# Where the weight tiles stand in SBUF against the matmuls' right sides: one pad for each stage, and the lower halves at two places in turn

## The chip, the cores and the metric

The kernel runs on one core of one Trainium2 chip. The metric is the device time of one execution in microseconds. The input is one sequence of 256 tokens, all in float32.

## The reference

Two layers, each of three sublayers with an adaptive norm in front: a feed-forward block, a mixer, a feed-forward block. The mixer of layer 0 is a hybrid (RG-LRU beside a chunked SSD), that of layer 1 is an mLSTM.

```python
for layer in range(2):
    mod = (silu(c) @ ada_w[layer] + ada_b[layer])        # shift, scale, gate of 3 sublayers
    h = modulate(x, 0)                                   # rms_norm, scale, shift
    x = x + 0.5 * (1 + gate0) * swiglu(h, w_gate, w_up, w_down)   # 1024 -> 2816 -> 1024
    h = modulate(x, 1)
    y = hybrid_mixer(h, ...) if layer == 0 else mlstm_block(h, ...)
    x = x + (1 + gate1) * y
    h = modulate(x, 2)
    x = x + 0.5 * (1 + gate2) * swiglu(h, ...)
return rms_norm(x, final_norm_g)
```

Nearly all the arithmetic is the product of 256 tokens with weights that are read once: the gate, up and down projections of four feed-forward blocks, and the input and output projections of the two mixers.

## The kernel before

All weights lie in DRAM as one stream of 128x128 tiles in the order of use, 2928 of them, in 366 pieces of 8 tiles (512 KB). `Weights._piece(i)` loads a piece (`wraw`, SP queue), rounds it on ScalarE to float32r (`whi`, the upper half) and subtracts on VectorE (`wlo`, the lower half, what the rounding left). It runs 4 pieces ahead of the use. Six buffers of each half go round in one pool. Activations are kept as two parts in the same way.

A product of a tile is three matmuls with the 256 tokens as columns: upper weights times upper tokens, upper times lower, lower times upper. Two forms exist, and this text calls them narrow and wide.

- Narrow (`multiply`, lines L333, L334, L335; the four output blocks that open a sublayer do the same with 258 columns in L380 to L382): each of the three has its own weight load (128 columns, `LDWEIGHTS`) and 256 columns. 2118 tiles: the gate and up projections (tile names `gu`, `gu_f`), all of the hybrid's (`bc`, `xbc`, `xl`, `z`, `ri`, `gl`, `od1`), the mLSTM's input (`up`, `zz`), and the last of the eight output blocks of the last sublayer.
- Wide (`out_project`, L438 and L440): the upper tile meets both parts of the tokens in one matmul of 512 columns, then the lower tile 256 columns. 810 tiles: the other output projections (`od0`, `od2`, `od3`, `od4`, `od5`; the digit is the sublayer).

The weight load of a matmul can run while the matmul ahead of it runs. In the text an offset is the address of the weight tile that is being loaded, less the address where the right side (the tokens' tile, `hb`, `ph`, `yb`, `ysb`, `ylb` or `xlb`) of the running matmul begins, in bytes within a partition, modulo 512. A tile's row is 512 bytes long and both parts of every right side begin at the same place modulo 512 (`LO_ROW` and the pads see to that), so all tiles of a stage have the same offset, whatever buffer they are in. Tiles named `pad` or `xpad` are never written or read; they only move what is allocated after them. `WIDE` lists the pieces whose lower half is shifted by 64 bytes (`o = 16` elements).

The scheduler of the framework sets the order on each engine, by priorities and by when buffers come free; `ADA_PLAN` spreads 144 further loads and products on VectorE (`ada`, the modulation) over the pieces.

Of the kernel before, what the change touches and what calls it, by code (L numbers as in the profile page):

```python
# [11 lines left out]
F32 = mybir.dt.float32  # L12
# [7 lines left out]
P = 128  # L20
# [36 lines left out]
WIDE = []  # L57
for _i, _n in enumerate((ND * NF, 0, ND * NF, ND * NF, ND * 16, ND * NF)):
    _e = sum(SUB_TILES[:_i + 1])
    WIDE.append(((_e - _n) // PIECE, _e // PIECE))  # L60
LO_ROW = 384


# [6 lines left out]
class Weights:  # L70
# [14 lines left out]
    def _piece(self, i):  # L85
        nc = self.nc
        w = PIECE * P
        raw = self.raw_pool.tile([P, w], F32, tag="wraw", name=f"wraw{i}")
        nc.sync.dma_start(raw, self.src[i])


        o = 16 if any(p <= i < q for p, q in WIDE) else 0
        hi = self.part_pool.tile([P, w], F32R, tag="whi", name=f"whi{i}")
        lo = self.part_pool.tile([P, w + 128], F32R, tag="wlo", name=f"wlo{i}")[:, o:o + w]
        with self.tc.high_priority(offset=self.ahead):
            if i < 2:
                raw_hi = nc.scalar.copy(hi, raw)
                if i == 1:
                    self.tc.add_manual_dep(raw_hi.ins, self.first[1].ins.name, NOSYNC, reason="the first input first")
            else:  # L100
                raw_hi = nc.scalar.copy(hi, raw)  # L101
            self.last = nc.vector.tensor_tensor(out=lo, in0=raw, in1=hi.bitcast(F32), op=ALU.subtract)  # L102
        if i < 2:
            self.tc.add_manual_dep(self.last.ins, self.first[0].ins.name, NOSYNC, reason="the first input first")
        self.parts[i] = (hi, lo)
        self.splits[i] = (raw_hi, self.last)
        for n, ins in self.after.pop(i, ()):
            self._behind(i, n, ins)
# [25 lines left out]
def body(ctx: ExitStack, tc: tile.TileContext, a, out, dbg=None):  # L134
# [4 lines left out]
    xp = ctx.enter_context(tc.tile_pool(name="xp", bufs=1))  # L139
# [30 lines left out]


    hb = xp.tile([P, ND, 2 * LO_ROW], F32R, name="hb")
    xp.tile([P, 48], F32, name="xpad")
    hh, hl = hb[:, :, 0:T + 2], hb[:, :, LO_ROW:LO_ROW + T + 2]
    h = [hb[:, k, 0:2 * LO_ROW].rearrange("p (i t) -> p i t", i=2)[:, :, 0:T] for k in range(ND)]
    hx = [(hh[:, k, :], hl[:, k, :]) for k in range(ND)]
# [16 lines left out]
    for b in range(2):  # L193
        q = fpool.tile([P, D], F32, name=f"xsq{b}")
# [616 lines left out]
    def mlstm_weights(pp, pw):  # L811
        NC = 16

        wc = pp.tile([P, 3, NC, 4], F32, name="wqkv")
        nc.gpsimd.dma_start(wc, a["ml_w"])
        wkr = pw.tile([P, NC, 4, 4], F32, name="wkr")
        nc.gpsimd.dma_start(wkr, a["ml_wkr"])
        bg = pp.tile([P, 8], F32, name="bg")
        nc.gpsimd.dma_start(bg, a["ml_bg"][0:1, :].to_broadcast([P, 8]))
        wqk = pp.tile([P, NC, 4], F32, name="wqk")  # L820
        pr = pw.tile([P, NC, 4, 4], F32, name="wqk_pr")
        nc.vector.tensor_tensor(out=pr, in0=wkr, in1=wc[:, 0].unsqueeze(2).to_broadcast([P, NC, 4, 4]), op=ALU.mult)
        nc.vector.tensor_reduce(out=wqk, in_=pr, axis=AX.X, op=ALU.add)
        wg = []
        for i in range(3):
            r = pw.tile([P, NC, 8, 4], F32, tag="wgr", name=f"wgr{i}")
            nc.gpsimd.dma_start(r, a["ml_wg"][i])
            nc.vector.tensor_tensor(out=r, in0=r, in1=wc[:, i].unsqueeze(2).to_broadcast([P, NC, 8, 4]), op=ALU.mult)
            g = pp.tile([P, NC, 8], F32, name=f"wg{i}")
            nc.vector.tensor_reduce(out=g, in_=r, axis=AX.X, op=ALU.add)  # L830
            wg.append(g)
        wcg, wvg = wg[0], wg[2]
        nc.vector.tensor_tensor(out=wcg, in0=wg[0], in1=wg[1], op=ALU.add)
        return wc, wqk, wcg, wvg, bg
# [214 lines left out]
    for s in range(6):  # L1049
        W.ahead = AHEAD[s]  # L1050
        kind = ("ffn", "hyb", "ffn", "ffn", "ml", "ffn")[s]
        if s == 3:
            pp = outer.enter_context(tc.tile_pool(name="mlp", bufs=1, reuse_waits="tile"))
        with ExitStack() as sc:
            if kind == "ffn":
                fp = sc.enter_context(tc.tile_pool(name=f"ffn{s}", bufs=NF, reuse_waits="tile"))
                fp.tile([P, 56 if s in (2, 5) else 48], F32, name=f"pad{s}", bufs=1)
                during = None
                if s == 3:
                    pw = sc.enter_context(tc.tile_pool(name="mlpw", bufs=1, reuse_waits="tile"))  # L1060
                    weights = []
                    during = lambda: weights.extend(mlstm_weights(pp, pw))
                ys = ffn(s, acc, fp, during)
            elif kind == "hyb":
                sp = sc.enter_context(tc.tile_pool(name="hyb", bufs=1, reuse_waits="tile"))
                sp.tile([P, 120], F32, name="pad1")
                wk = sc.enter_context(tc.tile_pool(name="hybw", bufs=8, reuse_waits="tile"))
                ys, beside = hybrid(s, acc, sp, wk)
            else:
                sp = sc.enter_context(tc.tile_pool(name="ml", bufs=1, reuse_waits="tile"))  # L1070
                sp.tile([P, 48], F32, name="pad4")
                wk = sc.enter_context(tc.tile_pool(name="mlw", bufs=16, reuse_waits="tile"))
                ys = mlstm(s, acc, sp, wk, weights)
            acc = out_project(s, ys, kind == "ffn", beside if kind == "hyb" else None)
        if s == 0:
            first.close()
        if s == 4:
            outer.close()
# [130 lines left out]
```

## Time and profile before

| | before |
|---|---|
| median of 3 runs | 1148.38 us (1145.75 to 1150.41) |
| the profiled execution | 1148.33 us, of which span 1146.6 |
| TensorE busy | 1124.3 us of the span, 98% |
| VectorE busy | 957.8 us, 84% |
| ScalarE busy | 642.6 us, 56% |
| DMA | 236 GB/s of HBM traffic over the span |
| granted TensorE clock, mean | 0.997 |

The span runs from the first to the last instruction; the time of an execution is a little longer. TensorE's matmuls are pipelined: a matmul shows 0.28 us although the next begins 0.12 us after it, so what counts is the distance between starts. The place of a row in the program is read from its line and from the names out<-in.

### The profile page before, as it was taken

The page shows a single profiled execution, that of the slowest core. Times are in us where ns is not written, and L with a number is a line of the kernel's source. Part 1 is how long each engine was busy: PE and PEld are TensorE (multiplying, and loading weights), DVE is VectorE, ACT ScalarE, POOL GpSimd, SP SyncE. Part 2 cuts the span into 40 slices and gives each one's busy share as a digit, 9 for nine tenths or more (in the row PEclk, how much of TensorE's full clock was granted, in tenths as well). Part 3 has the DMA queues.
Part 4 walks back from the last instruction along what each step waited for, and adds up shares of the span by engine and source line. Part 5 has one row for each costly group of instructions (what it writes and reads, how often), then busy time and mean ns, then how long its engine had stood idle before and what let it go on. Part 6 is the DMA issues. An engine that isn't in the chain of part 4 may idle for free.

```text
span 1146.6 us, 21903 instructions
## 1 busy us (share of the span) xinstructions
PE 1124.3 (98%) x8548; PEld 1072.7 (94%) x8548; DVE 957.8 (84%) x1831; ACT 642.6 (56%) x1074; POOL 8.6 (1%) x25
## 2 busy tenths in 40 slices
PE   7999999999999999999999999999999999999997
PEld 6999988999989999999899998889999889999987
DVE  7999899999889798788889888989879988766562
ACT  4465444788976565444554444458765456544452
POOL 0000000000000000000000000000000000000000
PEclk8999999999999999999999999999999999999999
DMA  8999989656655659899849899983532375875561
GB/s 319 349 305 367 373 294 334 204 172 201 198 166 170 203 196 328 297 313 309 276 150 322 291 336 346 328 270 110 156 120 75 117 239 158 266 227 189 183 198 42
DMA packets 75273, 272.25 MB, mean 237 GB/s; under 512 B 8449, under 2 KB 9121, under 8 KB 75170
## 3 DMA queue, kind: packets, MB, share of 16 engines
q1 hardware_dynamic: 74160, 268.99, 69.4%
q0 software_dynamic: 432, 1.10, 0.4%
q8 instruction: 67, 1.10, 0.4%
q10 hardware_dynamic: 578, 0.76, 0.2%
q14 instruction: 36, 0.29, 0.1%
HBM read 269.77 MB, written 1.05 MB: 236 GB/s over the span
## 4 chain that ended last, share of the span: by engine, by line
PE 84%; DVE 8%; DMA 4%; ACT 2%; issue 1%; ACTq 0%; DVEq 0%; SPq 0%
PE od L438 13%; PE gu L335 13%; PE gu L334 13%; PE gu L333 13%; PE od L440 7%; DMA wraw<-in_wst_dram 4%; DVE wlo L102 3%; ACT whi L101 1%; PE gu_f L380 1%; PE gu_f L382 1%; PE up L335 1%; PE up L334 1%; PE up L333 1%; PE gu_f L381 1%; PE od L333 1%
## 5 line engine op out<-in xcount | busy, mean ns | idle before, releaser
L101 ACT CAST whi<-wraw 128x1024 fp32r<-128x1024 f32 x364 | 380.6, 1049 | 289.1 <-DMA wraw<-in_wst_dram 164.8
L102 DVE TENSOR_TENSOR wlo<-wraw,whi 128x1024 fp32r<-128x1024 f32 x366 | 446.9, 1222 | 100.5 <-ACT whi L101 97.1
L334 PE MATMUL gu<-hb,whi 128*128 128x256 f32 x1312 | 365.9, 280 | 0.1
L335 PE MATMUL gu<-hb,wlo 128*128 128x256 f32 x1312 | 365.9, 280 | 0.0
L333 PE MATMUL gu<-hb,whi 128*128 128x256 f32 x1312 | 362.4, 280 | 1.5 <-ACT hb L349 1.5
L334 PEld LDWEIGHTS gu<-hb,whi 128*128 128x128 f32 x1312 | 246.9, 188 | 0.4 <-DVE hb L350 0.3
L335 PEld LDWEIGHTS gu<-hb,wlo 128*128 128x128 f32 x1312 | 246.8, 188 | 0.0
L333 PEld LDWEIGHTS gu<-hb,whi 128*128 128x128 f32 x1312 | 244.7, 188 | 2.0 <-ACT hb L349 2.0
L438 PE MATMUL od<-ph,whi 128*128 128x512 f32 x682 | 234.0, 391 | 2.4 <-DVE ph L327 2.4
L440 PE MATMUL od<-ph,wlo 128*128 128x256 f32 x682 | 189.0, 277 | 0.0
L219 DVE SCALAR_TENSOR_TENSOR ada<-ada,cact 128x1024 f32<-128x1024 f32 x144 | 175.0, 1219 | 0.1
L438 PEld LDWEIGHTS od<-ph,whi 128*128 128x128 f32 x682 | 128.1, 188 | 29.6 <-DVE ph L327 2.7
L440 PEld LDWEIGHTS od<-ph,wlo 128*128 128x128 f32 x682 | 128.0, 188 | 0.0
L326 ACT CAST ph<-fg 128x256 fp32r<-128x256 f32 x88 | 35.2, 406 | 89.7 <-DVE fg L469 89.4
L445 DVE SCALAR_TENSOR_TENSOR x<-od,gate,x 128x256 f32<-128x256 f32 x87 | 41.6, 481 | 23.0 <-PE od L440 11.8
L327 DVE TENSOR_TENSOR ph<-fg,ph 128x256 fp32r<-128x256 f32 x88 | 36.7, 422 | 12.3 <-ACT ph L326 12.3
L438 PE MATMUL od<-yb,whi 128*128 128x512 f32 x128 | 45.1, 396 | 0.0
L468 ACT ACTIVATE fg<-gu 128x256 f32<-128x256 f32 x82 | 30.6, 377 | 15.2 <-PE gu L335 15.1
L333 PE MATMUL zz<-hb,whi 128*128 128x256 f32 x128 | 37.4, 292 | 0.0
L335 PE MATMUL zz<-hb,wlo 128*128 128x256 f32 x128 | 37.0, 289 | 0.0
L334 PE MATMUL zz<-hb,whi 128*128 128x256 f32 x128 | 36.8, 287 | 0.0
L440 PE MATMUL od<-yb,wlo 128*128 128x256 f32 x128 | 36.0, 282 | 0.0
(407 smaller groups left out, 1887.8 us busy)
## 6 DMA issues: line engine op xcount, KB each, us to landing
wraw<-in_wst_dram SPq DMA_DIRECT2D x366, 512.0 KB, 4.3
ada<-in_adaT_dram SPq DMA_DIRECT2D x144, 512.0 KB, 5.4
xn<-in_x_dram SPq DMA_DIRECT2D x2, 512.0 KB, 4.0
wgr<-in_ml_wg_dram POOLq DMA_DIRECT2D x3, 256.0 KB, 5.7
out_dram<-res ACTq DMA_DIRECT2D x2, 128.0 KB, 2.3
out_dram<-res SPq DMA_DIRECT2D x2, 128.0 KB, 2.1
out_dram<-res SPq DMA_DIRECT2D x1, 256.0 KB, 2.5
out_dram<-res ACTq DMA_DIRECT2D x1, 256.0 KB, 2.6
```

The costliest lines, as they stand in the source:

```text
L101: raw_hi = nc.scalar.copy(hi, raw)
L102: self.last = nc.vector.tensor_tensor(out=lo, in0=raw, in1=hi.bitcast(F32), op=ALU.subtract)
L219: nc.vector.scalar_tensor_tensor(out=raw, in0=raw, scalar=1.0, in1=cact, op0=ALU.mult, op1=ALU.mult, accum_out=mods[s][:, m:m + 1])
L326: nc.scalar.copy(hi, src)
L327: nc.vector.tensor_tensor(out=both[:, 1, :], in0=src, in1=hi.bitcast(F32), op=ALU.subtract)
L333: m = nc.tensor.matmul(dst, wh, both[:, 0, :], start=start, stop=False, skip_group_check=True)
L334: nc.tensor.matmul(dst, wh, both[:, 1, :], start=False, stop=False, skip_group_check=True)
L335: nc.tensor.matmul(dst, wl, both[:, 0, :], start=False, stop=stop, skip_group_check=True)
L438: nc.tensor.matmul(bank, wh, both.rearrange("p i t -> p (i t)"), start=(k == 0), stop=False, skip_group_check=True)
L440: nc.tensor.matmul(sums[0], wl, both[:, 0, :], start=False, stop=(k == len(rhs) - 1), skip_group_check=True)
L445: nc.vector.scalar_tensor_tensor(out=xs_t[d], in0=part, scalar=g[:, d:d + 1], in1=xs_t[d], op0=ALU.mult, op1=ALU.add)
L468: nc.scalar.activation(g, b[:, 0:T], AF.Silu)
```

## The change

The pad behind the tokens' tile grows by 256 bytes, so that everything after it, the weights' buffers among it, moves by 256 bytes modulo 512. The hybrid's own pads follow, one of them new (`pad2`), which places the right side `xlb` like the others. The lower half gets a shift that depends on whether the piece's number is odd, and the last two pieces no longer count as wide.

```diff
 for _i, _n in enumerate((ND * NF, 0, ND * NF, ND * NF, ND * 16, ND * NF)):
     _e = sum(SUB_TILES[:_i + 1])
     WIDE.append(((_e - _n) // PIECE, _e // PIECE))
+WIDE[-1] = (WIDE[-1][0], WIDE[-1][1] - 2)
 LO_ROW = 384
@@ Weights._piece
-        o = 16 if any(p <= i < q for p, q in WIDE) else 0
+        o = 16 + 64 * (i % 2) + (0 if any(p <= i < q for p, q in WIDE) else 16)
         hi = self.part_pool.tile([P, w], F32R, tag="whi", name=f"whi{i}")
         lo = self.part_pool.tile([P, w + 128], F32R, tag="wlo", name=f"wlo{i}")[:, o:o + w]
@@ body
-    xp.tile([P, 48], F32, name="xpad")
+    xp.tile([P, 112], F32, name="xpad")
@@ body, the hybrid's pools
-                sp.tile([P, 120], F32, name="pad1")
+                sp.tile([P, 184], F32, name="pad1")
                 wk = sc.enter_context(tc.tile_pool(name="hybw", bufs=8, reuse_waits="tile"))
+                wk.tile([P, 104], F32, name="pad2", bufs=1)
```

The offsets in the built programs, in bytes modulo 512:

| matmuls | tiles | upper, before | upper, now | lower, before | lower, now (even, odd piece) |
|---|---|---|---|---|---|
| narrow, right side `hb`, `ysb`, `ylb` | 2080 | 192 | 448 | 192 | 64, 320 |
| narrow, right side `xlb` | 16 | 96 | 448 | 96 | 64, 320 |
| narrow, last output block, `ph` | 22 | 448 | 448 | 0 | 64, 320 (16 tiles); 256 (6 tiles) |
| wide, `ph` and `yb` | 810 | 448 | 448 | 0 | 0, 256 |

The number of instructions on each engine is the same, and the order on TensorE, VectorE and the SP queue too. The new pad takes the hybrid's small buffers off memory that was used earlier, and so three small instructions move. On ScalarE at the program's start (`cact` is the conditioning vector after Silu, `x` the transposed input, `dg` the first diagonal tile of the SSD's skip), before:

```order
L190 ACTIVATE cact<-c_107 128x512
L190 ACTIVATE cact<-c_110 128x512
L201 COPY x<-xT_118 128x512
L201 COPY x<-xT_124 128x512
L201 COPY x<-xT_130 128x512
```

and now, where `dg` waits for the column table `cols`:

```order
L191 ACTIVATE cact<-c_107 128x512
L191 ACTIVATE cact<-c_110 128x512
L754 ACTIVATE dg_3846<-ident,cols 128x128
L202 COPY x<-xT_118 128x512
L202 COPY x<-xT_124 128x512
L202 COPY x<-xT_130 128x512
```

The diagonal tile now stands ahead of the copies of x. Its old place on ScalarE is at the end of the first sublayer (`wdt`, `wdh` are the small weights of the SSD's time step), before:

```order
L101 CAST whi_2398<-wraw_2396 128x1024
L753 ACTIVATE dg_3845<-ident,cols 128x128
L316 ACTIVATE sq_o_7_2442<-x 128x256
L363 ACTIVATE hb<-x,scale_1922 128x256
L101 CAST whi_2420<-wraw_2418 128x1024
L619 ACT_TABLE_LOAD
L619 ACTIVATE hv<-hv 128x16
L101 CAST whi_2491<-wraw_2489 128x1024
L599 CAST wdh<-wdt 128x128
```

and now:

```order
L102 CAST whi_2398<-wraw_2396 128x1024
L600 CAST wdh<-wdt 128x128
L317 ACTIVATE sq_o_7_2442<-x 128x256
L364 ACTIVATE hb<-x,scale_1922 128x256
L102 CAST whi_2420<-wraw_2418 128x1024
L620 ACT_TABLE_LOAD
L620 ACTIVATE hv<-hv 128x16
L102 CAST whi_2492<-wraw_2490 128x1024
```

The cast of the small weights has taken the diagonal tile's place, since its load no longer waits. On GpSimd (POOL), whose queue issues that load, before:

```order
L204 AFFINE_SELECT tri<-ones 128x128
L595 DMA hv<-in_ssd_hv_dram 128x32
L597 DMA wdt<-in_wdt_dram 128x128
L638 MEMSET stk 48x256
L817 DMA wkr<-in_ml_wkr_dram 128x256
```

and now:

```order
L205 AFFINE_SELECT tri<-ones 128x128
L598 DMA wdt<-in_wdt_dram 128x128
L596 DMA hv<-in_ssd_hv_dram 128x32
L639 MEMSET stk 48x256
L818 DMA wkr<-in_ml_wkr_dram 128x256
```

The load of `wdt` has passed that of `hv`, which still waits for memory of the first sublayer, and so is issued at the program's start.

## The prediction

> **What bounds the kernel now.** I read the page's busy shares and the chain of work that ended last, then tables of busy time for chosen stretches, then single start times of matmuls in order of time.
>
> ```profile
> PE 1124.3 (98%) x8548; PEld 1072.7 (94%) x8548; DVE 957.8 (84%) x1831; ACT 642.6 (56%) x1074; POOL 8.6 (1%) x25
> ...
> PE 84%; DVE 8%; DMA 4%; ACT 2%; issue 1%; ACTq 0%; DVEq 0%; SPq 0%
> ```
>
> TensorE is busy for 98% of the span and makes 84% of the chain: the time is a count of matmuls times the distance from one start to the next. So the question is that distance. By stage, for the matmuls of one tile name alone (stretch, its length, then TensorE's busy time with the number of matmuls; the last three columns are granted clock, DMA share and GB/s):
>
> ```profile
> 70.00:130.00 60.00, 60.00 (x512) 60.00 (x511) 4.59 (x11) 4.17 (x11) 1.00 0.98 367
> 980.00:1070.00 90.00, 90.00 (x767) 90.00 (x766) 6.66 (x16) 6.01 (x16) 1.00 0.69 219
> ```
> ```profile
> 150.00:190.00 40.00, 40.00 (x230) 35.06 (x229) 5.08 (x11) 1.00 0.95 336
> 530.00:570.00 40.00, 40.00 (x237) 35.52 (x236) 4.81 (x10) 1.00 0.88 301
> 915.00:945.00 30.00, 30.00 (x173) 26.23 (x172) 5.58 (x12) 1.00 0.74 228
> ```
>
> The first two are narrow matmuls (256 columns) of the feed-forward layers: 60/512 is 117 ns each and 90/767 is 117 ns, at clock 1.00, whether the DMA share is 0.98 or 0.69. The other three are wide pairs (512 then 256 columns): 40/230 is 174 ns a matmul, 348 ns a pair; 40/237 is 169 ns, 338 a pair; 30/173 is 347 a pair. The same program line with equal offsets modulo 512 takes two different times in different stages at the same clock. Single starts show it. Narrow, first the usual spacing, then a shorter one:
>
> ```profile
> 979.16 0.28 PE L333 MATMUL gu<-hb,whi 128*128 128x256 f32 x1
> 979.28 0.28 PE L334 MATMUL gu<-hb,whi 128*128 128x256 f32 x1
> 979.39 0.28 PE L335 MATMUL gu<-hb,wlo 128*128 128x256 f32 x1
> 979.51 0.28 PE L333 MATMUL gu<-hb,whi 128*128 128x256 f32 x1
> ```
> ```profile
> 965.11 0.28 PE L333 MATMUL gu<-hb,whi 128*128 128x256 f32 x1
> 965.23 0.28 PE L334 MATMUL gu<-hb,whi 128*128 128x256 f32 x1
> 965.34 0.28 PE L335 MATMUL gu<-hb,wlo 128*128 128x256 f32 x1
> 965.45 0.28 PE L333 MATMUL gu<-hb,whi 128*128 128x256 f32 x1
> ```
>
> A tile's three matmuls take 0.35 us there and 0.34 here; over longer stretches 353 ns (3 x 117.7) and 340 (3 x 113.3). Wide, the first output projection and the second feed-forward's:
>
> ```profile
> 160.14 0.28 PE L440 MATMUL od<-ph,wlo 128*128 128x256 f32 x1
> 160.26 0.40 PE L438 MATMUL od<-ph,whi 128*128 128x512 f32 x1
> 160.49 0.28 PE L440 MATMUL od<-ph,wlo 128*128 128x256 f32 x1
> ```
> ```profile
> 560.21 0.28 PE L440 MATMUL od<-ph,wlo 128*128 128x256 f32 x1
> 560.33 0.39 PE L438 MATMUL od<-ph,whi 128*128 128x512 f32 x1
> 560.55 0.28 PE L440 MATMUL od<-ph,wlo 128*128 128x256 f32 x1
> ```
>
> 350 ns a pair against 340, to the end of each stage. So there is a loss of about 4 ns in a narrow matmul and 10 in a pair, which comes and goes with the phase in which a weight load meets the running matmul. The change moves that meeting, nothing else.
>
> **The change part by part.**
>
> *Order.* TensorE, VectorE and the SP queue keep their order to the instruction. Three small ones move, since the pad takes the hybrid's buffers off older ones. On ScalarE the first diagonal tile (0.40 us) goes from 202.03 to the start, between the second Silu and the first copy of x, and waits there for the column table:
>
> ```profile
> 1.34 5.08 DMA cols<-in_cols_dram
> 6.23 0.60 ACT L190 ACTIVATE cact<-c 128x512 f32<-128x512 f32 x1 [1.11 <-PE c L189]
> 7.27 0.59 ACT L201 COPY x<-xT 128x512 f32<-128x512 f32 x1 [0.45 <-PE xT L200]
> 202.03 0.40 ACT L753 ACTIVATE dg<-ident,cols 128x128 f32<-128x128 f32 x1
> wdt<-in_wdt_dram POOLq DMA_DIRECT2D x1, 64.0 KB, 4.2
> ```
>
> The table lands at 6.42, the Silu ends at 6.83, the copy starts at 7.27: 0.40 fits into 0.44, cost 0. If the table landed late, its lateness would stand in front of the copies, which the first matmuls need. The cast of the small weights moves up into the place that the tile left. On POOL the load of wdt (64 KB) passes that of hv and so starts at about 1.8 us, beside the table's load (226 KB, in the 5.08 us above): 64/226 of that, 1.4 us, is the bound above, 0 the one below; I take 0.2, since the table is only one of many loads then in flight.
>
> *Wide tiles* (810). Upper offset stays 448; the lower goes from 0 to 0 and 256 in turn. Bounds: the two stages at 350 (304 tiles) go to 340, -3.0 us; the three at 340 (506 tiles) go to 350, +5.1. I take 0, because both spacings hold with these offsets now.
>
> *Narrow tiles* (2118, of which 2096 stood at 192 for both halves, 16 of them at 96). Now upper 448, lower 64 and 320. The nearest rows with the upper at 448 are the 22 tiles of the very last output block, which are narrow and had upper 448, lower 0:
>
> ```profile
> 1132.23 0.28 PE L333 MATMUL od<-ph,whi 128*128 128x256 f32 x1
> 1132.35 0.28 PE L334 MATMUL od<-ph,whi 128*128 128x256 f32 x1
> 1132.47 0.28 PE L335 MATMUL od<-ph,wlo 128*128 128x256 f32 x1
> 1132.59 0.28 PE L333 MATMUL od<-ph,whi 128*128 128x256 f32 x1
> 1132.70 0.28 PE L334 MATMUL od<-ph,whi 128*128 128x256 f32 x1
> 1132.82 0.28 PE L335 MATMUL od<-ph,wlo 128*128 128x256 f32 x1
> 1132.94 0.28 PE L333 MATMUL od<-ph,whi 128*128 128x256 f32 x1
> 1133.05 0.28 PE L334 MATMUL od<-ph,whi 128*128 128x256 f32 x1
> 1133.16 0.28 PE L335 MATMUL od<-ph,wlo 128*128 128x256 f32 x1
> 1133.29 0.28 PE L333 MATMUL od<-ph,whi 128*128 128x256 f32 x1
> ```
>
> The next weights load while a matmul runs. Under L333 the load at 448 runs: 0.12, 0.11, 0.11, mean 113 ns, the free value. Under L334 the load at 0: 0.12, 0.12, 0.11, mean 117. Under L335 again 448: 0.12, 0.12, 0.13, mean 123. Sum 353, as at 192. Unlike there, the losses are not even: upper after upper is free, and the loss sits at the lower load and the one behind it. In the wide pairs of 340 the load at 448 runs under a narrow matmul without loss (560.21 to 560.33). So I take 448 as a place that costs nothing unless the lower load before it has upset the phase, and 0 as one that does. For 64 and 320 no row exists. Bounds for a tile: 3 x 113.3 = 340 with no loss anywhere; 113 + 123 + 123 = 359 with the longest step at the lower load and its successor. I take 344.6, two free steps and one lower step of 118, the mean of 113 and 123: of all values seen under a narrow matmul it is the usual one. That is 8.6 ns less than 353.2.
>
> *How much reaches the end.* 1312 tiles of the feed-forward loop (164 output blocks of 8) and 96 that open it run with TensorE always busy: 1408 x 8.6 ns = 12.1 us. The other 688, in the hybrid and the mLSTM, stand in stretches where TensorE waits for others too (tables of all instructions; columns TensorE, weight loads, VectorE, ScalarE):
>
> ```profile
> 64.00:137.00 73.00, 73.00 (x623) 73.00 (x621) 69.45 (x110) 38.09 (x59) 0.00 (x0) 1.00 0.98 359
> 203.00:372.00 169.00, 165.01 (x1350) 156.90 (x1349) 153.60 (x349) 135.22 (x265) 0.00 (x0) 1.00 0.59 185
> ```
>
> VectorE is busy for 153.60 of 169.00 there; I count half, 3.0 us. What is late next is supply: in 64 to 137 VectorE is busy for 69.45 of 73 and the DMA engines for 0.98. A stretch shorter by 8.6/353 would be 71.2, VectorE at 98%; I take 1.1 us off for waits that then show. Sum: -12.1 - 3.0 + 1.1 + 0.2 = -13.8. The profiled execution took 1148.33 us (span 1146.6 and 1.73 around it), the median of the runs is 1148.38, so no correction: 1134.5, in round numbers 1135.
>
> What can be told from no change is about 0.5%, 5.7 us: the three runs before span 4.7.
>
> **The rivals.**
>
> *Nothing to tell (1148).* Every meeting costs the same on average wherever it falls. For it: 192 gives 353 a tile, 448 with 0 gives 353, and 96 gives no less (the first and last of five starts in a row, three rows left out):
>
> ```profile
> 302.39 0.28 PE L334 MATMUL ri<-xlb,whi 128*128 128x256 f32 x1
> ...
> 302.87 0.28 PE L335 MATMUL ri<-xlb,wlo 128*128 128x256 f32 x1
> ```
>
> 0.48/4 is 120. Against it: 340 exists in the same rows, so the average isn't forced. Its time is 1148.3 + 0.2, with up to -3.0 or +5.1 from the wide tiles, still inside 0.5%. A rule gives the same time by another way: the Trainium skill, "TensorE: Matmul & The Clock Gate", Part 2, the step on LDWEIGHTS, says that loading the next tile's weights takes no SBUF read bandwidth from the running matmul, as the two have ports of their own. By it no address would matter, and no loss should come and go; of the 0.27 below, I give 0.05 to this reason alone. The trace doesn't bear that out: the 128x512 matmul takes 0.40 us at 160.26 and 0.39 at 560.33, at one clock.
>
> *All free (1118).* The two lower places keep the phase where it costs nothing, everywhere: 2096 x 13.2 ns = 27.7 us if the hybrid's share counts fully, and 3.0 of the wide tiles: 1148.3 - 30.7. For it: steps of 113 ns are seen at 965 even with offsets that usually lose them. Against: supply, by the 69.45 of 73.
>
> *Slower (1159).* One mechanism: the lower load at 64 or 320 meets the matmul at its worst, and the upper load behind it starts out of phase, as under L335 in the last block. Both steps then take 122 and the first 114, 358 a tile: 2096 x 4.9 = 10.3 us. It decides from 355.9 a tile on (5.7 us/2096 tiles above 353.2). For it: 0.13 at 1133.16, with lower at 0. Against: these rows then begin each tile with a free step, which makes up for it.
>
> *The change not taking effect* is excluded: the built program holds every narrow upper load at 448 past its right side.
>
> **How the numbers follow.** Forecast 0.36, all free 0.14, nothing 0.27, slower 0.23. Faster by over 0.5% is the first two, 0.50; within 0.27; slower 0.23. The forecast's own range comes from the lower step: at 123 a tile takes 349.6, 3.6 less, and the same sum ends at 1142; at 115 it takes 341.6 and ends at 1129. Since cases of both signs hold most of the chance, the range runs from all free, 1117, to just past slower, 1160; I leave out about 0.12, for tiles above 358 (up to the bound of 359) together with wide tiles that turn slow, and for a late column table on top.
>
> **What the profile of the changed kernel would show.** Right: matmuls of 60 us of the feed-forward loop rise from 512 towards 525 (512 x 353.2/344.6), with steps of 0.11 under L334 (then L335) and more under the lower load only. All free: 530 or more. Nothing: 510 to 514. Slower: fewer than 508, with the longest steps at the lower load. Wide: pairs of 340 or 350; a switch at every eighth tile would show that the two lower places differ. The start is right if the diagonal tile stands in the gap before 7.27 and the copy of x has not moved. Wrong would be the forecast if 64 and 320 act unlike each other, one free and one at the worst, since a mean over pieces then hides both, or if VectorE in the first layer can't follow.

## The result and the profile after

| | before | after |
|---|---|---|
| median of 16 runs each | 1148.02 us (1144.45 to 1151.9) | 1142.61 us (1133.27 to 1146.1) |
| ratio after/before, 95% interval | | 0.9937, 0.9913 to 0.9961 |
| the profiled execution, and its span | 1148.33 us, 1146.6 | 1143.54 us, 1141.8 |

The change makes the kernel faster by 0.63%, 5.4 us. Two readings of the profile matter: the gain is not spread over all narrow tiles, and one part of it is given back. First the page's lines that answer to those of before, busy shares and chain:

```profile
PE 1116.2 (98%) x8548; PEld 1064.0 (93%) x8548; DVE 957.6 (84%) x1831; ACT 642.6 (56%) x1074; POOL 8.7 (1%) x25
...
PE 73%; DVE 14%; DMA 6%; ACT 4%; issue 3%; ACTq 0%; SPq 0%
```

TensorE's share of the chain fell from 84% to 73%, VectorE's rose from 8% to 14%: at some place TensorE now waits for others. The same span by sublayer, each from the start of its first matmul to the start of the next sublayer's first (the last one to the end of the span):

| | before, us | after, us | difference |
|---|---|---|---|
| up to the first weight matmul | 15.03 | 14.56 | -0.47 |
| 1, feed-forward | 188.29 | 187.03 | -1.26 |
| 2, hybrid | 187.48 | 188.69 | +1.21 |
| 3, feed-forward | 189.95 | 191.03 | +1.08 |
| 4, feed-forward | 188.43 | 189.37 | +0.94 |
| 5, mLSTM | 183.19 | 181.15 | -2.04 |
| 6, feed-forward | 194.23 | 189.97 | -4.26 |

(The program counts sublayers from 0, so sublayers 1, 3, 4 and 6 of this table have the tile names `gu0`/`od0`, `gu2`/`od2`, `gu3`/`od3` and `gu5`/`od5`. From here on I use these names.)

In this execution nearly all of the gain comes from the last sublayer. Tables of busy time for the `gu` matmuls alone say why (stretch, length, TensorE's busy time with the count of matmuls, then weight loads, VectorE, ScalarE, clock, DMA share, GB/s). Before, in `gu0`, `gu2`, `gu3` and `gu5`:

```profile
30.00:130.00 100.00, 100.00 (x851) 100.00 (x851) 7.49 (x19) 6.91 (x19) 1.00 0.96 350
430.00:500.00 70.00, 70.00 (x597) 70.00 (x596) 4.98 (x12) 4.89 (x13) 1.00 0.90 314
610.00:690.00 80.00, 80.00 (x682) 80.00 (x681) 5.39 (x13) 4.87 (x13) 1.00 0.90 317
980.00:1060.00 80.00, 80.00 (x682) 80.00 (x681) 5.82 (x14) 5.26 (x14) 1.00 0.70 225
```

and after:

```profile
30.00:130.00 100.00, 99.93 (x852) 99.74 (x851) 7.50 (x19) 6.80 (x19) 1.00 0.94 345
430.00:500.00 70.00, 70.00 (x591) 70.00 (x590) 4.98 (x12) 4.88 (x13) 1.00 0.87 311
610.00:690.00 80.00, 80.00 (x708) 80.00 (x707) 5.39 (x13) 4.85 (x13) 1.00 0.90 321
980.00:1060.00 80.00, 80.00 (x709) 80.00 (x707) 6.22 (x15) 5.62 (x15) 1.00 0.68 228
```

Before, each loop has one matmul in 117 ns. After, `gu3` and `gu5` have one in 113 (80/708), but `gu2` has one in 118.4 (70/591), at the same offsets, clock and program line. Single starts show the two spacings. In `gu2`:

```profile
439.76 0.28 PE L334 MATMUL gu<-hb,whi 128*128 128x256 f32 x1
...
440.48 0.28 PE L334 MATMUL gu<-hb,whi 128*128 128x256 f32 x1
```

Six steps, 0.72 us, 120 ns. In `gu3`:

```profile
640.06 0.28 PE L334 MATMUL gu<-hb,whi 128*128 128x256 f32 x1
...
640.74 0.28 PE L334 MATMUL gu<-hb,whi 128*128 128x256 f32 x1
```

Six steps, 0.68 us, 113 ns. The mean distance of the starts is 118.9 ns in `gu2` from its third piece on (the first two contain waits), and 113.4 over the whole of `gu3` and `gu5`. `gu0` changes over within the loop: it runs at 113.3 from its sixth piece to an interruption in its fifteenth, and at 118.9 from there to its end. Even and odd pieces, so lower at 64 and at 320, do not differ in either.

`gu3` is 4.2 us shorter than before (108.71 us, was 112.95), and the output projection behind it, `od3`, is 5.2 longer (67.59, was 62.41). The list of waits of TensorE, and its starts in order of time:

```profile
PE od L439 <- DVE ph L328: 5.7, 2, 3.3
```
```profile
709.31 0.28 PE L441 MATMUL od<-ph,wlo 128*128 128x256 f32 x1
711.99 0.56 PE L439 MATMUL od<-ph,whi 128*128 128x512 f32 x1 [2.40 <-DVE ph L328]
712.34 0.41 PE L441 MATMUL od<-ph,wlo 128*128 128x256 f32 x1
716.09 0.79 PE L439 MATMUL od<-ph,whi 128*128 128x512 f32 x1 [3.33 <-DVE ph L328]
716.68 0.41 PE L441 MATMUL od<-ph,wlo 128*128 128x256 f32 x1
716.90 0.63 PE L439 MATMUL od<-ph,whi 128*128 128x512 f32 x1
```

TensorE stands idle for 5.7 us (2.4 in before), waiting for the token parts `ph` of the next output rows. Then it runs at half the clock: a wide matmul takes 0.63 us instead of 0.39, and the table gives the granted clock beside it:

```profile
712.60:719.00 6.40, 3.07 (x10) 2.52 (x10) 5.74 (x9) 2.32 (x5) 0.00 (x0) 0.50 0.92 294
```

What `ph` waits for on its way stands in the rows of ScalarE and VectorE just ahead: the rounding of a piece waits for its load, the lower half waits for the rounding, and the tokens' parts stand behind it in VectorE's order.

```profile
707.81 1.05 ACT L102 CAST whi<-wraw 128x1024 fp32r<-128x1024 f32 x1 [2.63 <-DMA wraw<-in_wst_dram]
```
```profile
708.89 1.23 DVE L103 TENSOR_TENSOR wlo<-wraw,whi 128x1024 fp32r<-128x1024 f32 x1 [1.31 <-ACT whi L102]
```

So the place where the kernel got faster is followed by one that waits for its supply, and the wait costs twice, once as idle time and once as half clock. The first output projection, `od0`, went from 61.48 us to 59.74 (a wide pair in 340 ns instead of 350); `od2`, `od4` and `od5` kept theirs within 0.2 us.

### The profile page after: what moved, and what is told of

It reads as the page before. It is cut to its first block, busy times and chain, and to the rows that moved or that the text cites. A ratio compares the mean times of both kernels' runs of the same rounds, so it can differ in the third digit from the quotient of the medians.

```text
span 1141.8 us, 21905 instructions
## 1 busy us (share of the span) xinstructions
PE 1116.2 (98%) x8548; PEld 1064.0 (93%) x8548; DVE 957.6 (84%) x1831; ACT 642.6 (56%) x1074; POOL 8.7 (1%) x25
## 4 chain that ended last, share of the span: by engine, by line
PE 73%; DVE 14%; DMA 6%; ACT 4%; issue 3%; ACTq 0%; SPq 0%
PE od L439 15%; PE gu L335 9%; PE gu L334 9%; PE gu L336 9%; PE od L441 8%; DVE wlo L103 5%; DMA wraw<-in_wst_dram 5%; DVE ada L220 3%; ACT whi L102 2%; DVE hb L351 1%; DMA wgr<-in_ml_wg_dram 1%; PE od L334 1%; PE up L335 1%; PE up L336 1%; DVE ht L348 1%
## 5 line engine op out<-in xcount | busy, mean ns | idle before, releaser
L335 PE MATMUL gu<-hb,whi 128*128 128x256 f32 x1312 | 365.8, 280 | 0.1
L334 PE MATMUL gu<-hb,whi 128*128 128x256 f32 x1312 | 360.2, 279 | 1.6 <-ACT hb L350 1.5
L334 PEld LDWEIGHTS gu<-hb,whi 128*128 128x128 f32 x1312 | 245.1, 189 | 2.3 <-ACT hb L350 2.1
L335 PEld LDWEIGHTS gu<-hb,whi 128*128 128x128 f32 x1312 | 246.8, 188 | 0.3 <-DVE hb L351 0.3
L328 DVE TENSOR_TENSOR ph<-fg,ph 128x256 fp32r<-128x256 f32 x88 | 36.7, 422 | 12.9 <-ACT ph L327 12.8
L334 PE MATMUL zz<-hb,whi 128*128 128x256 f32 x128 | 37.2, 290 | 0.0
L335 PE MATMUL zz<-hb,whi 128*128 128x256 f32 x128 | 36.8, 288 | 0.0
L350 ACT ACTIVATE hb<-ht,shift 128x256 fp32r<-128x256 f32 x48 | 22.6, 505 | 24.2 <-DVE ht L348 24.2
```

Source lines behind the costliest of these rows:

```text
L328: nc.vector.tensor_tensor(out=both[:, 1, :], in0=src, in1=hi.bitcast(F32), op=ALU.subtract)
L334: m = nc.tensor.matmul(dst, wh, both[:, 0, :], start=start, stop=False, skip_group_check=True)
L335: nc.tensor.matmul(dst, wh, both[:, 1, :], start=False, stop=False, skip_group_check=True)
```

## The experiments

Three questions: which part of the change makes the gain, what decides between 113 and 118 ns, and what `od3` waits for. Places are offsets as in the table of the change. Each experiment's runs were compared with runs of the kernel before on the same chip; loops are read from one profiled execution of each.

### Without the turn between two places (lo_one_place)

```diff
-        o = 16 + 64 * (i % 2) + (0 if any(p <= i < q for p, q in WIDE) else 16)
+        o = 16 if any(p <= i < q for p, q in WIDE) else 32
```

> The changed kernel with the lower halves at one place (64 narrow, 0 wide) instead of two in turn; upper stays at 448. Theory of the lock (with the upper at 448 a narrow stage keeps one of two spacings, 113.3 or 118.9 ns, from its beginning on, and the turn between places has no part in it): each of the four feed-forward loops shows one of these two values, time 1133 to 1146, median within 4 us of the changed kernel. Rival, the turn frees the stage: without it every loop stays at one value of 117.7 or more, time 1147 or more.

Measured: 1140.31 us against 1149.65, ratio 0.9931 (0.9911 to 0.9951). `gu3` and `gu5` take 108.71 us as with the change, `gu2` 114.68, `gu0` 122.72 (126.70 with the change). The gain is there without the turn. The theory that a loop keeps its spacing from its beginning on fails in `gu0`, which went from 113 to 119 and back to 113.

### Without the move of the upper weights (upper_192)

The pads of before, the lower weights as in the change:

```diff
-    xp.tile([P, 112], F32, name="xpad")
+    xp.tile([P, 48], F32, name="xpad")
-                sp.tile([P, 184], F32, name="pad1")
+                sp.tile([P, 120], F32, name="pad1")
-                wk.tile([P, 104], F32, name="pad2", bufs=1)
```

> The changed kernel with the three pads of before: upper narrow loads at 192 again, lower at 320 and 64 in turn, wide as in the changed kernel. Theory that the upper place matters: no feed-forward loop keeps 113.3, all are at 117.5 to 118, time 1147 to 1150. Rival, the lower place matters: loops at 113.3 appear as in the changed kernel, time 1133 to 1146.

Measured: 1139.31, ratio 0.9926 (0.99 to 0.9952). The `gu` rows:

```profile
30.00:130.00 100.00, 99.91 (x876) 99.45 (x875) 7.49 (x19) 6.97 (x20) 1.00 0.97 349
430.00:500.00 70.00, 70.00 (x620) 70.00 (x619) 5.25 (x13) 4.49 (x12) 1.00 0.89 311
```

876 where before had 851, 620 where it had 597. The move of the upper weights from 192 to 448, which the prediction built on, is not needed: upper 192 with lower 64 and 320 gives as much. What the change and this run share is the new place of the lower weights. The two upper places are 256 bytes apart, so this run does not say that the upper place is without effect; the scans below take other ones.

### Modulation loads spread out (ada_spread)

```diff
-    (2, (6, 60), range(64, 96)), (3, (6, 60), range(96, 136)), (5, (6, 40), range(136, 144)),
+    (2, (4, 64), range(64, 100)), (3, (1, 66), range(100, 136)), (5, (6, 40), range(136, 144)),
```

Four of the 40 loads of sublayer 3 go to sublayer 2, and the other 36 are spread out.

> The changed kernel with the modulation loads of sublayers 2 and 3 spread thinner (36 each over 60 and 65 pieces instead of 32 and 40 over 54). Theory of supply (the loop of sublayer 3 at 113.3 outruns its weights, and the output projection behind it gives the gain back): the wait of TensorE at the start of that projection falls from 5.7 us to under 2.5 and the half clock behind it is gone, also where the loop runs at 113.3; median 2 us or more under the changed kernel. Rival, the wait comes from the order of the evacuation alone: it stays above 5 us where the loop is at 113.3, median as the changed kernel's.

Measured: 1138.44, ratio 0.991 (0.9877 to 0.9944). `od3` takes 59.73 us behind a `gu3` at 113.4 ns, with no wait inside and no half clock. But the four blocks that open that sublayer take 15.24 us, 2.9 longer: that early loads are in the way there is an argument, not shown. The interval overlaps that of the change (0.9913 to 0.9961), so that this version beats it is not shown either, nor whether the loads or VectorE's products of them had been late.

### The places one after the other (scan1, scan2, scan3)

The right side is moved inside its row so that each sublayer has another upper place; the lower place moves on every five pieces:

```diff
+SCAN = ((124, 2), (190, 3), (304, 5))
+        for p, s in SCAN:
+            if p <= i < p + 40:
+                o = ((64 * ((i - p) // 5)) - 448 + 4 * SHIFT[s]) % 512 // 4
```

scan1 has the upper at 448, 0 and 192 in `gu2`, `gu3` and `gu5`, scan2 at 64, 320 and 128; scan3 has it at 192 in all three and moves the lower by 32 bytes, by 8, and by 64 in falling order.

> The changed kernel with the right side shifted within its row and the lower halves moved every 5 pieces, in three feed-forward loops: upper at 448 in sublayer 2, at 0 in sublayer 3, at 192 in sublayer 5, and in each the lower at 0, 64, 128 up to 448, 5 pieces each. Theory that the upper place decides: with 448 spacings of 113.3 appear for several lower places, with 192 none lasts (117 to 119 throughout), with 0 unknown. Rival, the pair of places decides: single lower places give 113.3 in each of the three loops. Rival, places don't matter and only chance does: each loop keeps one spacing over all its lower places.

> Right side shifted by sublayer so that the upper stands at 64 (sublayer 2), 320 (3), 128 (5); the lower moves on by 64 bytes every five pieces, from 0 to 448. Theory (period of 256 bytes, equal places 117.8): the pattern repeats after four places in each loop, 320 reads like 64, and the place equal to the upper gives 117.8. Rival (distance modulo 512 matters): 64 and 320 differ. One-look time about 1140 to 1150.

> Upper at 192 in all three loops. Sublayer 2: lower in steps of 32 bytes from 0 to 224; sublayer 3: in steps of 8 from 32 to 88; sublayer 5: in steps of 64 in falling order, 448 to 0. Theory (the place sets the spacing, history only draws between two): sublayer 5 gives 113.3 or 118.9 at 320 and 64, 117.8 or 115.5 at 384 and 128, 117.8 elsewhere; within 32 bytes around 64 nothing changes. Rival (the order in which places come sets the spacing): falling order gives other values at the same places, up to 120.

Measured (one execution each): 1143.2, 1144.6 and 1144.8 us. The rows of scan1 for the upper at 192, with the lower at 64, 128 and 192 (12 us each):

```profile
974.00:986.00 12.00, 12.00 (x108) 12.00 (x107) 0.83 (x2) 0.75 (x2) 1.00 0.82 268
988.00:1000.00 12.00, 12.00 (x106) 12.00 (x106) 0.83 (x2) 0.79 (x3) 1.00 0.78 252
1002.00:1014.00 12.00, 12.00 (x104) 12.00 (x104) 0.83 (x2) 0.76 (x2) 1.00 0.66 219
```

and of scan2 for the upper at 64, with the lower at 128, 192, 256 and 448:

```profile
436.00:448.00 12.00, 12.00 (x104) 12.00 (x104) 0.83 (x2) 0.75 (x2) 1.00 0.82 302
450.00:462.00 12.00, 12.00 (x108) 12.00 (x107) 0.83 (x2) 0.75 (x2) 1.00 0.94 333
464.00:476.00 12.00, 12.00 (x105) 12.00 (x103) 0.83 (x2) 0.78 (x3) 1.00 0.89 308
506.00:518.00 12.00, 12.00 (x109) 12.00 (x108) 0.83 (x2) 0.74 (x2) 1.00 0.91 317
```

A count of 12 us is good to one in a hundred only; the mean distance of the starts over the last four pieces of a place gives, in ns a matmul, with both places taken modulo 256 (the first place of `gu2` without the piece that contains waits):

| upper | lower 0 | lower 64 | lower 128 | lower 192 |
|---|---|---|---|---|
| 0 | 120.0 | 117.8 | 119.1 | 117.8 |
| 64 | 117.8 | 117.8 | 118.2 | 113.3 |
| 128 | 118.3 | 117.8 or 118.7 | 118.7 | 116.7 or 120.0 |
| 192 | 117.8 | 113.3 or 118.9 | 115.5 or 117.8 | 117.8 |

The first theory of scan1, that the upper place decides, is refuted: in its loops the upper at 448 had 113.3 at no lower place, and the upper at 192 had it at two. Nor does the distance of the two places alone decide, since upper 0 with lower 128 and upper 64 with lower 192 are equally far apart and take 119.1 and 113.3; both count, from the right side.

In scan2 `gu2` (upper 64) and `gu3` (upper 320) have the same mean in each of their last 35 pieces, to a tenth of a nanosecond, so 256 bytes make no difference there. `gu5` (upper 128) does not bear the theory out: lower places 256 bytes apart gave 117.8 and 118.7 (64 and 320), 116.7 and 120.0 (192 and 448). Whether 256 bytes matter there or the loop entered these places differently is not told apart.

The other two cells with two values, upper 192 with lower 64 and with lower 128, had them at exactly the same offsets in different loops: 113.3 in `gu5` of scan1 and 118.9 in scan3, 115.5 and 117.8. So a pair of places does not always fix the spacing. In scan3 the falling order gave the values of the rising one at every place but three, all in these two cells: lower at 320 and 64 took 118.9 (113.3 in scan1), and lower at 128 took 117.8 (115.5). That the order decides, as the rival had it, is not shown, because `gu2` of scan3, in rising order, took 118.9 at 64 too. From 32 to 88 in steps of 8 every place but 64 gave 117.8, and 64 gave 118.9, so the expectation that nothing changes there was wrong: 8 bytes beside 64 the spacing is another.

The pair of upper 64 with lower 192 (modulo 256) is the only one that went to 113.3 all four times it was met, each time out of a spacing of 117.8 or more.

### The two halves at one place modulo 256 (same_place)

The change, with the narrow lower weights at 192 and 448 in turn:

```diff
-        o = 16 + 64 * (i % 2) + (0 if any(p <= i < q for p, q in WIDE) else 16)
+        o = 64 * (i % 2) + (16 if any(p <= i < q for p, q in WIDE) else 64)
```

> The changed kernel with the narrow lower weights at 192 and 448 in turn, so that they stand at the upper weights' place modulo 256. Theory (what counts is the distance of the two places modulo 256, and the upper place alone does nothing): the gain goes; narrow steps 117.8 ns in all three feed-forward loops (112.9 us each), od3 about 62.4, time 1148 (1144 to 1152). Rival (upper 448 itself is the gain): 113.4 in one or two loops, 1139 to 1143 as with the change.

Measured: 1148.31 against 1148.17, ratio 1.0001 (0.9983 to 1.0019). The gain is gone with the upper weights still at 448. The order of the instructions on every engine is that of the change, so the place of the lower weights is the cause. In the profiled execution, at 1146.0 us the shortest of ten, `gu0` stands at 117.8 after its start, and of the other loops `gu2` alone kept 113:

```profile
430.00:500.00 70.00, 70.00 (x620) 70.00 (x619) 4.98 (x12) 4.85 (x13) 1.00 0.89 313
610.00:690.00 80.00, 80.00 (x682) 80.00 (x681) 5.41 (x13) 4.89 (x13) 1.00 0.87 317
980.00:1060.00 80.00, 80.00 (x682) 80.00 (x681) 5.82 (x14) 5.63 (x15) 1.00 0.66 220
```

So equal places, too, can hold 113 through a loop: the theory's step from equal places to 117.8 is right for two of its three loops, and what the places set is a tendency there.

### Upper 192 and a gentler spread (both)

upper_192 with `(2, (5, 64), range(64, 99)), (3, (5, 66), range(99, 136))` in `ADA_PLAN`.

> Upper 192 with lower 320 and 64 in turn (so the pads of before), and the modulation vectors of sublayers 2 and 3 given out over pieces 5 to 64 and 5 to 66, where they stood over 6 to 60. Theory: a loop draws 113.4 or 118.9, and with the vectors spread od3 keeps 60 us after a short gu3 loop instead of 67; 1134 to 1142, 1137 expected, below the change alone by 2 to 5. Rival (the supply is short anyway, the spread only moves the wait): od3 stays at 66 or od2 or the opening of sublayer 3 grows by as much, 1139 to 1143.

Measured: 1142.36, ratio 0.9954 (0.9937 to 0.9972), at the rival's end. `gu2`, `gu3` and `gu5` are at 113.4, but `od3` waits 4.1 us and takes 65.71, `od2` takes 63.37 (59.75 with the change) and the opening of `gu3` 13.76. Loads moved by a few pieces only moved the wait here; what ada_spread gained in `od3` did not come back here.

### What od3 waits for (ada_no_load, ada_short)

The change, once without the 40 loads of modulation weights of the sublayer of `od3`, once with the loads but a short product:

```diff
-        nc.sync.dma_start(raw, a["adaT"][b])
+        src = cact if 96 <= b < 136 else raw
+        if src is raw:
+            nc.sync.dma_start(raw, a["adaT"][b])
```
```diff
+        n = 16 if 96 <= b < 136 else D
-        nc.vector.scalar_tensor_tensor(out=raw, in0=raw, scalar=1.0, in1=cact, ...
+        nc.vector.scalar_tensor_tensor(out=raw[:, 0:n], in0=raw[:, 0:n], scalar=1.0, in1=cact[:, 0:n], ...
```

> The changed kernel without the 40 loads of modulation weights in sublayer 3 (it multiplies another vector in their place, times zero, so that part of the computation is left out; VectorE's instructions stay). Theory (the loads are what is late in od3: the DMA engines are the limit): after a gu3 loop of 108.7 us od3 takes 60 instead of 67.6, no half clock there, about 1135. Rival (VectorE is the limit): od3 stays at 66 to 68, about 1143.

> The changed kernel with VectorE's multiplication of the 40 modulation weights of sublayer 3 cut to 16 of 1024 columns (that part of the computation is left out); their loads stay. VectorE's work there falls by 40 x 1.1 us. Rival (VectorE is the limit): od3 60, about 1135. Theory (DMA): od3 stays at 66 to 68, about 1143.

Measured: 1135.2 and 1143.9 us. In both `gu3` takes 108.71 us as with the change. `od3` takes 59.73 us without the loads and 65.83 with the short product. ScalarE's waits for the weights' load in the 52 us up to the stall, without the loads and with the short product (total, times, longest):

```profile
ACT whi L102 <- DMA wraw<-in_wst_dram: 2.1, 3, 1.2
```
```profile
ACT whi L102 <- DMA wraw<-in_wst_dram: 15.2, 12, 3.5
```

With the change it was 10.6 in 9 times. The stretches of `od3` (all instructions; columns TensorE, weight loads, VectorE, ScalarE, POOL, clock, DMA share, GB/s), in the same order:

```profile
702.00:762.00 60.00, 60.00 (x357) 53.08 (x355) 50.54 (x77) 28.91 (x38) 2.57 (x4) 1.00 0.66 220
```
```profile
705.00:771.00 66.00, 63.26 (x355) 55.07 (x354) 44.52 (x85) 31.39 (x42) 2.61 (x4) 0.97 0.86 308
```

Without the loads VectorE has its full work, 50.54 of 60, and nobody waits. So the loads are needed for the stall. That VectorE's products have no part is not shown. With the short product its busy time falls to 44.52 of 66, and TensorE still waits for `ph`, but 2.7 us in place of 5.7. Waits and half clock (what the wide pairs longer than 360 ns took beyond 340, added up) cost `od3` 7.9 us with the change, 2.7 in before and 4.6 here; another 1.5 of the 65.83 us are later wide pairs at 350 ns in place of 340. The rows of VectorE with the change show how the two meet. From 708.89, the end of its wait for the late rounding shown above, it works without idle time until it has made the second `ph` that TensorE waits for. A product stands right ahead of that one, as another did at 710.36 ahead of the first:

```profile
714.47 1.22 DVE L220 SCALAR_TENSOR_TENSOR ada<-ada,cact 128x1024 f32<-128x1024 f32 x1
715.62 0.42 DVE L328 TENSOR_TENSOR ph<-fg,ph 128x256 fp32r<-128x256 f32 x1
```

Late loads start the stall, and VectorE then works off what has piled up. The wait is named after VectorE, since `ph` is made there behind the halves of late weights.

### The pair that returns (upper_320)

The change with pads smaller by 32 elements, so the upper at 320 and the lower at 192 and 448, which modulo 256 is 64 and 192:

```diff
-    xp.tile([P, 112], F32, name="xpad")
+    xp.tile([P, 80], F32, name="xpad")
-                sp.tile([P, 184], F32, name="pad1")
+                sp.tile([P, 152], F32, name="pad1")
```

> Upper weights 320 bytes past the right side in place of 448, lower at 192 and 448 in turn (pads smaller by 32 floats); modulo 256 that is 64 and 192, the pair that went to 113.3 in both loops where the lower had been moved there. Theory (this pair leads back to 113.3 from wherever it starts, the change's pair holds whichever it starts in): 113.3 in all feed-forward loops and the first layer 122.7 us, od3 again 66 to 68; time 1134 (1130 to 1139), below the change alone, and a narrower spread of runs. Rival (also drawn at the start of a loop): loops at 118 or more in some stages, 1139 to 1145.

Measured: 1136.54 against 1146.51, ratio 0.9927 (0.9903 to 0.9952).

```profile
30.00:130.00 100.00, 99.90 (x873) 99.21 (x872) 7.46 (x19) 7.24 (x20) 1.00 0.96 347
430.00:500.00 70.00, 70.00 (x620) 70.00 (x620) 4.96 (x12) 4.88 (x13) 1.00 0.90 314
610.00:690.00 80.00, 80.00 (x708) 80.00 (x707) 5.78 (x14) 5.22 (x14) 1.00 0.89 324
980.00:1060.00 80.00, 80.00 (x708) 80.00 (x708) 6.20 (x15) 5.62 (x15) 1.00 0.68 221
```

All four loops are at 113. In `gu0` two pieces were thrown to 118 and the pieces behind them came back to 113; with the change the same loop, once thrown from 113 to 119, stayed there to its end, and in lo_one_place, at the change's pair, it was thrown from 119 to 113 and stayed there. `od3` gives 4.6 us back again (66.97), 1.5 of it because its wide pairs ran at 350 ns in place of 340 behind the wait. The runs range over 9.1 us, with the change over 12.8, which is not the narrow band I expected. The intervals of the two ratios overlap, so the time does not show that this pair beats the change's. The loops speak for it: in upper_320 and late_eight all four are at 113.3. Of the seven profiled executions at the change's pair modulo 256 (the change, lo_one_place, upper_192, ada_spread, both, ada_no_load, ada_short) `gu3` and `gu5` came to 113.3 in all, `gu2` in three, and `gu0` ended there in three.

### Eight loads later (late_eight)

upper_320, with `(3, (6, 62), range(96, 128)), (4, (10, 28), range(128, 136))` in `ADA_PLAN`: eight of the 40 loads go to the mLSTM.

> Upper weights at 320, lower at 192 and 448 in turn, and eight of the 40 modulation loads of sublayer 3 given to sublayer 4 (32 over pieces 6 to 62 there, eight over pieces 10 to 28 of the mLSTM, which has DMA shares of 0.3 to 0.5). Theory (the loads of the modulation weights are what od3 is late by): od3 60 to 62 us instead of 67, the mLSTM 0 to 3 longer for eight more instructions on VectorE (10 us there), time 1131 (1128 to 1137). Rival (the mLSTM's VectorE pays it all back): od3 60, the mLSTM longer by 6 or more, 1136 to 1140.

Measured: 1134.46 against 1150.16, ratio 0.9895 (0.9855 to 0.9935), the lowest time of all. `od3` takes 64.55 (66.97 in upper_320), with one wait:

```profile
PE od L439 <- DVE ph L328: 3.1, 1, 3.1
```

and the mLSTM, from its first matmul to the next sublayer's first, 184.45 us (180.75 in upper_320). So between these two executions `od3` gains 2.4 and the mLSTM loses 3.7. Of the 2.4, 1.5 are wide pairs back at 340 ns, and of the 3.7 about 1.3 are the wide pairs of `od4`, 350 ns in place of 340, so less than half of the gain belongs to the loads. The better ratio cannot be put down to them.

## Why the prediction was right, and where its steps failed

The forecast was 1135 with 1117 to 1160, and 0.50 for faster. The time, 1142.61, is in the range and faster by more than 0.5%. The sum was -13.8 us and came to -4.8 in the profiled execution (-5.4 in the medians). That it came out faster is in part luck: the range of 43 us held the time of every rival, and the gain came from the lower weights' place, for which the prediction had no row, and not from the upper's, on which it built.

*What bounds the kernel* held: the time is a count of matmuls times the distance of their starts, that distance is 113 or about 118 ns at one clock, and it follows the places of the weights (same_place against the change: ratios to before of 1.0001 and 0.9937, from the lower weights' place alone).

*Upper 448 as the free place* failed. upper_192 has as much gain with the upper left at 192, and same_place has none with it at 448. The step was read from three tiles of the last output block of before, whose steps under L333, L334 and L335 are 113, 117 and 123 ns. Over all its 22 tiles they are 115, 118 and 121: under L333 steps of 113 and 117 alternate in a pattern at one pair of offsets. So 113 was not the price of a load at 448; by the scans it is the pair of places that counts.

*The lower step at 118, so 344.6 ns a tile* is the term that was mis-sized, and its form was wrong. No loop has 344.6. A loop that keeps one spacing has 340 (3 x 113.4) or 357 (3 x 118.9), and the 525 matmuls in 60 us that were to show the step right came in no loop: by 80/708 it is 531, by 70/591 it is 507. The rule that losses belong to loads, which the prediction took from rows, would have one spacing per pair of places; the scans show two at the same offsets in two of the 16 cells, and same_place in a third. The feed-forward loops gained 7.0 us (0.5 and 0.9 lost in `gu0` and `gu2`, 4.2 and 4.2 gained in `gu3` and `gu5`) where 12.1 stood.

*Half of the hybrid's and the mLSTM's tiles, -3.0*: the two sublayers came to -0.8 together (+1.21 and -2.04).

*Supply takes 1.1 back, in the first layer*: the mechanism was right and both place and size wrong. It took 5.2 in `od3`. In the first sublayer, mostly at 113 ns a matmul in upper_192, `gu0` shrinks to 122.73 and `od0` keeps 59.73, so nothing is given back there, where VectorE had 69.45 of 73. (The hybrid behind it took 191.05 us in that execution and 188.09 in upper_320, so whether it gives something back is open.) VectorE's share of a stretch was not enough to read. The stall goes with the loads, and with VectorE's products short 2.7 us of wait are left; 0.90 of DMA over a loop does not show how late the last load is.

*Wide tiles, 0 within -3.0 to +5.1*: `od0` gained 1.7, the others nothing, and `od2` takes 350 a pair in upper_192 and 340 with the change; either spacing comes, as was said.

*The moved instructions* did what the working says. ScalarE's rows of the start:

```profile
6.22 0.60 ACT L191 ACTIVATE cact<-c 128x512 f32<-128x512 f32 x1 [1.11 <-PE c L190]
6.72 0.39 ACT L754 ACTIVATE dg<-ident,cols 128x128 f32<-128x128 f32 x1
7.27 0.59 ACT L202 COPY x<-xT 128x512 f32<-128x512 f32 x1 [0.16 <-PE xT L201]
```

The diagonal tile stands in the gap and the copy at 7.27 has not moved; the first weight matmul is 0.47 earlier, not 0.2 later. lo_one_place, with the same order, has it at 15.18, later than before (15.03), so a difference of this size says nothing.

Of the rivals, "all free" was half the truth: the free spacing is there through two of the four loops of the profiled execution, and which loops get it differs between executions of the same pair. The rival that every meeting costs the same is refuted by one pair of runs: same_place and the change differ in no instruction, only in where the lower weights stand, and have ratios of 1.0001 and 0.9937 to before. The Trainium skill, "TensorE: Matmul & The Clock Gate", Part 2, the step on LDWEIGHTS, says that loading the next tile's weights takes no SBUF read bandwidth from the running matmul. What the prediction drew from it, that no address would matter, is not borne out by these two runs; whether it is read bandwidth that is lost, no run here shows.

What stays open: why upper 64 with lower 192 comes back to 113 and the same two places exchanged do not always, what sets the spacing at a loop's start, and whether 256 bytes are a period for every pair, and by what part of the memory. No experiment here separates these.

## What to carry to other kernels

When identical matmuls are spaced differently in different loops, compare starts of one line across stages before pricing a change: here a pair of addresses allowed two lasting spacings, and a price per load read from one place was wrong. Scan the offsets with one kernel that moves them every few pieces, look for the pair that comes back to the short spacing after each interruption, and check it at several loops. A loop that gets shorter brings the next wait forward: take the loads away and the products away in two runs, and see what each is worth.

## What the runs showed of the hardware that I had not expected

- The spacing of 256-column matmuls with a weight load each depends on where the weights lie. Places 256 bytes apart acted alike in 35 of 35 pieces (upper 64 against 320, scan2). Eight bytes count: with the upper at 192, lower at 56 or 72 gave 117.8 ns, and 64 between them 118.9 in the same loop and 113.3 in another.
- One program at one pair of places has two lasting spacings, 113.3 and 118.9 ns, each through nearly a whole loop of 109 or 115 us.
- The clock fell to half behind short waits of TensorE. In upper_320 one wait of 4.12 us was followed by 3 us with a mean clock of 0.58 (the third number from the end), and in ada_short one of 2.75 by matmuls of 0.63 us:

```profile
706.00:709.00 3.00, 3.00 (x11) 2.54 (x11) 3.00 (x5) 1.96 (x2) 0.00 (x0) 0.58 0.94 335
```

```profile
715.24 0.50 PE L440 MATMUL od<-ph,whi 128*128 128x512 f32 x1 [2.75 <-DVE ph L329]
...
716.20 0.63 PE L440 MATMUL od<-ph,whi 128*128 128x512 f32 x1
```

  In before a wait of 2.39 at the same place left the clock alone (the next wide matmul but one takes 0.39 again):

```profile
715.94 0.50 PE L438 MATMUL od<-ph,whi 128*128 128x512 f32 x1 [2.39 <-DVE ph L327]
...
716.74 0.39 PE L438 MATMUL od<-ph,whi 128*128 128x512 f32 x1
```

  With the change the first of two waits, 2.40, was followed by the half clock, so the length of a single wait does not decide it. The record of the granted clock shows what differs. Within each trace its changes lie whole multiples of 3.41 us apart. With the change the 2.40 us fall into one such stretch, 708.87 to 712.28, and the half clock begins at 712.28; in before the 2.39 us are cut at 715.39, with 1.84 in one stretch and 0.55 in the next. The Trainium skill, "TensorE: Matmul & The Clock Gate", section on HAM oscillation, has gaps of more than about 3.4 us as what to avoid; in these traces gaps of 2.40 and 2.75 us were enough.
